# A batched matmul on one core: PSUM tiles at fixed banks, and one row of a store moved between DMA engines

## The chip, the cores and the metric

One core of a Trainium2 chip. The metric is the device time of one execution in microseconds (us), median of several; the profile's span is about 1.8 us shorter than the timed execution it belongs to.

## The reference

```python
# x: 32 x 256 x 512 fp32, y: 32 x 512 x 384 fp32
def reference(x, y):
    return np.einsum('bij,bjk->bik', x, y).astype(np.float32)
```

## The kernel before

The 32 batches go in eight groups of four. For each group the kernel loads x (2 MB) and y (3 MB), rounds both to fp16 and transposes x on VectorE, multiplies on TensorE, copies the result out of PSUM (mostly on ScalarE) and stores 1.5 MB. The order of the parts is a fixed plan (x and y are loads, T rounds and transposes x, R rounds y, M multiplies, C and D copy the result out on ScalarE and VectorE, S stores), and all DMAs are issued from one queue, that of the sync engine. In the code below cuts are marked with `...`, and some statements that stand on several lines are joined.

```python
PLAN = """
x0 x1 y0
T0 x2 y1
...                                             # cut
T6 D4 R5 M5 C5 y7
T7 D5 R6 M6 C6 R7 M7 C7 D7 S3 S4 S5 S6 S7
"""
...
    psum_pool = ctx.enter_context(
        tc.tile_pool(name="psum", bufs=2 * Q, space=bass.MemoryType.PSUM)    # Q = 4: eight tiles
    )
...
    def multiply(n):
        ...
        for e in range(NE):                     # NE = 2
            for g in range(Q):
                ps_of[n, e, g] = psum_pool.tile([P, K], F32, name="o_ps")
            for t in range(T):                  # T = 16
                for g in range(Q):
                    s = slice(g * PQ, (g + 1) * PQ)
                    keep(nc.tensor.matmul(ps_of[n, e, g], xt[s, e, t // 2, :, t % 2], y_r[s, t],
                                          start=(t == 0), stop=(t == T - 1)))
...
    def store(n):
        w = width(n)
        per = P // w
        o = o_of.pop(n).rearrange("p (u f) k -> p u f k", u=Q // per)
        for u in range(Q // per):
            b = n * Q + u * per
            keep(nc.sync.dma_start(
                out=out[b : b + per].rearrange("g (s f) k -> (g s) f k", s=w), in_=o[:, u]))
```

A store of groups 0 to 5 is one DMA: 128 partitions, from each a run of eight rows of 384 fp32 (8 x 1.5 KB = 12 KB). Groups 6 and 7 are stored in two DMAs each, of 6 KB runs.

Of the kernel before, what the change touches and what calls it, by code (L numbers as in the profile page):

```python
# [1 line left out]

# [4 lines left out]


MM_DT = mybir.dt.float16
F32 = mybir.dt.float32  # L10
P = 128


Q = 4
STEP = 4
O_BUFS = 5
WIDE_GROUPS = 6



# [4 lines that stand above are left out]
T1 R0 M0 C0 x3 y2  # L25
T2 D0 R1 M1 C1 x4 y3 S0
T3 D1 R2 M2 C2 x5 y4 S1
T4 D2 R3 M3 C3 x6 y5
T5 D3 R4 M4 C4 x7 y6 S2
T6 D4 R5 M5 C5 y7  # L30
T7 D5 R6 M6 C6 R7 M7 C7 D7 S3 S4 S5 S6 S7
"""


@with_exitstack
def kernel(
    ctx: ExitStack,
    tc: tile.TileContext,
    x: bass.AP,
    y: bass.AP,  # L40
    out: bass.AP,
):
    nc = tc.nc

    B, I, J = x.shape
    _, _, K = y.shape

    PQ = P // Q
    R = I // PQ
    T = J // PQ  # L50
    TW = T // 2
    NE = I // P
    N = B // Q

    x_pool = ctx.enter_context(tc.tile_pool(name="x_pool", bufs=2))
    y_pool = ctx.enter_context(tc.tile_pool(name="y_pool", bufs=2))
    xr_pool = ctx.enter_context(tc.tile_pool(name="xr_pool", bufs=1))
    xt_pool = ctx.enter_context(tc.tile_pool(name="xt_pool", bufs=3))
    yr_pool = ctx.enter_context(tc.tile_pool(name="yr_pool", bufs=2))
    o_pool = ctx.enter_context(tc.tile_pool(name="o_pool", bufs=O_BUFS))  # L60
    psum_pool = ctx.enter_context(
        tc.tile_pool(name="psum", bufs=2 * Q, space=bass.MemoryType.PSUM)
    )

    keep = tc.keep_in_program_order




    x_of, y_of, xt_of, yr_of, ps_of, o_of = {}, {}, {}, {}, {}, {}  # L70

    def width(n):
        return PQ if n < WIDE_GROUPS else 2 * PQ

    def on_vector(n, e, g):
        if n < WIDE_GROUPS:
            return (e, g) == (NE - 1, Q - 1)
        return n == N - 1 and g % 2 == 1

    def load_x(n):  # L80
        x_of[n] = x_pool.tile([P, R, J], F32, name="x_sb")
        keep(
            nc.sync.dma_start(  # L83
                out=x_of[n],
                in_=x[n * Q : (n + 1) * Q].rearrange("g (p r) j -> (g p) r j", r=R),
            )
        )

    def load_y(n):
        y_of[n] = y_pool.tile([P, T, K], F32, name="y_sb")  # L90
        keep(
            nc.sync.dma_start(
                out=y_of[n],
                in_=y[n * Q : (n + 1) * Q].rearrange("g (q t) k -> (g q) t k", t=T),
            )
        )

    def transpose_x(n):


        x_r = xr_pool.tile([P, R, J], MM_DT, name="x_r")
        keep(nc.vector.tensor_copy(x_r, x_of.pop(n)))  # L102
        xt_of[n] = xt_pool.tile([P, NE, TW, P], F32, name="xt_sb")
        b = width(n) // PQ
        src = x_r.bitcast(F32).rearrange("p (b h e) (q t) -> p b e t h q", b=b, e=NE, t=TW)
        dst = xt_of[n].rearrange("p e t (h s b) -> p b e t h s", s=PQ, b=b)
        for e in range(NE):
            for c in range(b):
                keep(nc.vector.transpose(dst[:, c, e], src[:, c, e]))  # L109

    def round_y(n):
        y_sb = y_of.pop(n)
        yr_of[n] = yr_pool.tile([P, T, K], MM_DT, name="y_r")
        for a in range(0, T, STEP):
            keep(nc.vector.tensor_copy(yr_of[n][:, a : a + STEP], y_sb[:, a : a + STEP]))  # L115

    def multiply(n):
        xt = xt_of.pop(n).bitcast(MM_DT).rearrange("p e t (m c) -> p e t m c", c=2)
        y_r = yr_of.pop(n)
        o_of[n] = o_pool.tile([P, R, K], F32, name="o_sb")  # L120
        for e in range(NE):
            for g in range(Q):
                ps_of[n, e, g] = psum_pool.tile([P, K], F32, name="o_ps")
            for t in range(T):
                for g in range(Q):
                    s = slice(g * PQ, (g + 1) * PQ)
                    keep(
                        nc.tensor.matmul(  # L128
                            ps_of[n, e, g],
                            xt[s, e, t // 2, :, t % 2],  # L130
                            y_r[s, t],
                            start=(t == 0),
                            stop=(t == T - 1),
                        )
                    )

    def collect(n, vector):
        w = width(n)
        per = P // w
        copy = nc.vector.tensor_copy if vector else nc.scalar.copy  # L140
        o = o_of[n].rearrange("p (u f) k -> p u f k", u=Q // per)
        for e in range(NE):
            for g in range(Q):
                if on_vector(n, e, g) != vector:
                    continue
                ps = ps_of.pop((n, e, g))
                a = g % per * w
                for h in range(per):
                    keep(copy(o[a : a + w, g // per, h * NE + e], ps[h * w : (h + 1) * w]))  # L149
# [4 lines that stand above are left out]
        o = o_of.pop(n).rearrange("p (u f) k -> p u f k", u=Q // per)  # L154
        for u in range(Q // per):
            b = n * Q + u * per
            keep(
                nc.sync.dma_start(  # L158
                    out=out[b : b + per].rearrange("g (s f) k -> (g s) f k", s=w),
                    in_=o[:, u],  # L160
                )
            )

    parts = {
        "x": load_x,
        "y": load_y,
        "T": transpose_x,
        "R": round_y,
        "M": multiply,
        "C": lambda n: collect(n, False),  # L170
        "D": lambda n: collect(n, True),
        "S": store,
    }
    for step in PLAN.split():
        parts[step[0]](int(step[1:]))


# [1 line left out]
_INS = ['x', 'y']  # L179
_OUTS = [((32, 256, 384), 'float32')]  # L180


# [23 lines left out]
```

## Time and profile before

| | before |
|---|---|
| median of 3 runs, us | 135.07 (135.02 to 135.42) |
| busiest engine | VectorE (DVE), 72% of the span |
| data DMA queue, of 16 engines' span | 96.8% |
| moved by that queue | 54.5 MB |

How to read it: here the DMA engines are full from the second slice to the last but one (share 1.01 from 10 to 120 us), so the time is bytes over rate (54.5 MB at 409 GB/s are 133.3 us), and that share stood although the compute engines waited (TensorE 59.8 us for VectorE). But the sixteen DMA engines don't stop together. The mean share hides which of them ends last, and the last one sets the end: the last landing is at 132.30 us, and the sync engine's wait of 7.1 us ends there. The landing times of a DMA (sixteen for one of 128 partitions, read here as one for each engine, when its share of the data has arrived) show that. Below, an engine's lateness is its landing time after that of the first engine of the same DMA, and the spread is the lateness of the last. In this trace the spread, once there, stays: 2.54 us in the load that lands from 88.4 us, 2.53 in the last store, from 129.8. And the instruction transfers share the engines with the data: between 20 and 110 us 16 data packets are in flight at 91% of the moments without such a transfer, and 15 at 91% of those with one.

### The profile page before, as it was taken

What the parts mean: (1) busy time and instruction counts of PE and PEld (TensorE: products, weight loads), DVE (VectorE), ACT (ScalarE), POOL (GpSimd) and SP (SyncE); (2) the same over time, 40 slices, a digit from 0 to 9 for tenths busy, and PEclk for the clock granted to TensorE, in tenths of its full rate; (3) what the DMA queues carried; (4) which work ended last, traced back from release to release, by engine and by line L of the source; (5) the groups of instructions that cost most, each with busy time, mean ns of one, the idle gap of its engine ahead of it and who ended that gap; (6) DMA issues with size and microseconds to landing.
All of it is one profiled execution on the core that took longest, in us unless ns stands there. A gap on an engine that the chain in (4) does not pass through costs nothing.

```text
span 133.3 us, 2445 instructions
## 1 busy us (share of the span) xinstructions
PE 60.5 (45%) x1024; PEld 37.4 (28%) x1024; DVE 96.1 (72%) x92; ACT 91.5 (69%) x193; POOL 0.2 (0%) x4
## 2 busy tenths in 40 slices
PE   0000004970398039907980079700992298787000
PEld 0000002540255025503550045400560296444000
DVE  0049999699969999999069990899999940765300
ACT  3000000099999999999999993999959999997200
POOL 0000000000000000000000000000000000000000
PEclk9999999998569855995599555995599658999655
DMA  5999999989999999999999999999999999999992
GB/s 103 433 413 443 450 425 408 489 384 440 411 462 443 391 443 408 417 407 443 435 430 418 431 404 450 440 425 428 472 391 388 479 428 391 424 439 411 411 409 94
DMA packets 3755, 54.68 MB, mean 410 GB/s; under 512 B 416, under 2 KB 416, under 8 KB 928
## 3 DMA queue, kind: packets, MB, share of 16 engines
q1 hardware_dynamic: 3744, 54.53, 96.8%
q8 instruction: 8, 0.13, 0.4%
q14 instruction: 3, 0.02, 0.0%
HBM read 41.94 MB, written 12.58 MB: 409 GB/s over the span
## 4 chain that ended last, share of the span: by engine, by line
DMA 39%; DVE 21%; PE 16%; ACT 14%; issue 1%; DVEq 0%; SPq 0%
DMA x_sb<-in_x_dram 39%; PE o_ps L128 16%; ACT o_sb L149 14%; DVE xt_sb L109 7%; DVE o_sb L149 6%; DVE x_r L102 5%; DVE y_r L115 2%; DVEq L201 0%; SPq L158 0%; DVEq L102 0%; SPq L83 0%
## 5 line engine op out<-in xcount | busy, mean ns | idle before, releaser
L149 ACT COPY o_sb<-o_ps 32x384 f32<-32x384 f32 (+1 forms) x192 | 90.2, 470 | 31.9 <-PE o_ps L128 27.4
L128 PE MATMUL o_ps<-y_r,xt_sb 32*128 32x384 f16 x1024 | 60.5, 396 | 61.8 <-DVE y_r L115 59.8
L128 PEld LDWEIGHTS <-xt_sb 32*128 32x128 f16 x1024 | 37.4, 112 | 84.6 <-issue 52.6
L115 DVE CAST y_r<-y_sb 128x1536 f16<-128x1536 f32 x32 | 28.5, 953 | 6.1 <-DMA y_sb<-in_y_dram 5.9
L102 DVE CAST x_r<-x_sb 128x4096 f16<-128x4096 f32 x8 | 18.4, 2294 | 19.3 <-DMA x_sb<-in_x_dram 19.2
L109 DVE STREAM_TRANSPOSE xt_sb<-x_r 128x1024 f32<-128x1024 f32 (+1 forms) x20 | 31.6, 1627 | 0.3
L149 DVE COPY o_sb<-o_ps 32x384 f32<-32x384 f32 (+1 forms) x32 | 17.8, 556 | 2.9 <-PE o_ps L128 1.4
L149 ACT ACT_TABLE_LOAD x1 | 1.3, 1283 | 0.7 <-PEq L190 0.7
L190 POOL MEMSET const-bfloat16-1.0<- 128x1 bf16 x1 | 0.1, 103 | 0.0
L190 POOL MEMSET const-uint8-127<- 128x1 uint8 x1 | 0.1, 101 | 0.0
L190 POOL MEMSET const-float32-0.0<- 128x1 f32 x1 | 0.1, 98 | 0.2 <-issue 0.2
L190 POOL MEMSET const-float32-1.0<- 128x1 f32 x1 | 0.1, 98 | 0.0
## 6 DMA issues: line engine op xcount, KB each, us to landing
y_sb<-in_y_dram SPq DMA_DIRECT2D x8, 3072.0 KB, 22.3
x_sb<-in_x_dram SPq DMA_DIRECT2D x8, 2048.0 KB, 22.4
out_dram<-o_sb SPq DMA_DIRECT2D x6, 1536.0 KB, 23.7
out_dram<-o_sb SPq DMA_DIRECT2D x4, 768.0 KB, 8.4
```

The lines of the kernel that those rows point to most:

```text
L102: keep(nc.vector.tensor_copy(x_r, x_of.pop(n)))
L109: keep(nc.vector.transpose(dst[:, c, e], src[:, c, e]))
L115: keep(nc.vector.tensor_copy(yr_of[n][:, a : a + STEP], y_sb[:, a : a + STEP]))
L128: nc.tensor.matmul(ps_of[n, e, g], xt[s, e, t // 2, :, t % 2], y_r[s, t], start=(t == 0), stop=(t == T - 1),)
L149: keep(copy(o[a : a + w, g // per, h * NE + e], ps[h * w : (h + 1) * w]))
L190: nc = _bacc.Bacc("TRN2", target_bir_lowering=False, num_devices=1)
```

## The change

The intent: PSUM tiles are bound to fixed banks in place of a rotating pool, and in the store of group 5 (the sixth) some bytes are moved from six DMA engines to ten others.

```diff
+UNEVEN = 5
...
-        tc.tile_pool(name="psum", bufs=2 * Q, space=bass.MemoryType.PSUM)
+        tc.tile_pool(name="psum", bufs=1, space=bass.MemoryType.PSUM)
...
+    bank = {
+        (e, g): psum_pool.tile([P, K], F32, name=f"o_ps_{e}_{g}") for e in range(NE) for g in range(Q)
+    }
...
-                ps_of[n, e, g] = psum_pool.tile([P, K], F32, name="o_ps")
+                ps_of[n, e, g] = bank[e, g]
...
+            dst = out[b : b + per].rearrange("g (s f) k -> (g s) f k", s=w)
+            if n != UNEVEN:
+                keep(nc.sync.dma_start(out=dst, in_=o[:, u]))
+                continue
+
+            keep(nc.sync.dma_start(out=dst[:, : R - 1], in_=o[:, u, : R - 1]))
+            keep(nc.sync.dma_start(out=dst[:100, R - 1], in_=o[:100, u, R - 1]))
+            keep(nc.sync.dma_start(out=dst[100:, R - 1], in_=o[100:, u, R - 1]))
```

The traces number no engine, so the numbers 0 to 15 are names: 0 to 9 for the ten engines on which the DMA of 100 partitions lands, 10 to 13 for the four more of the fourteen on which the DMA of 28 partitions lands, 14 and 15 for the other two. That a name means the same engine in another run is assumption.

More of the change, by code (lines that the diff above doesn't have):

```diff
@@ L156, in store @@
             b = n * Q + u * per
-            keep(
-                nc.sync.dma_start(
-                    out=out[b : b + per].rearrange("g (s f) k -> (g s) f k", s=w),
-                    in_=o[:, u],
-                )
-            )
+            dst = out[b : b + per].rearrange("g (s f) k -> (g s) f k", s=w)
[5 more added lines that the diff above has]
+            keep(nc.sync.dma_start(out=dst[100:, R - 1], in_=o[100:, u, R - 1]))
     parts = {
```

## The prediction

> **What bounds the kernel now.** I read the page first, for the engines and for the DMA row, then the table by stretch (busy time by window) over the whole run and finely over its end, then the wait lists and the order in which the DMAs are issued, and last the trace's own records of DMA packets and of landings.
>
> The page of the kernel before:
>
> ```profile
> span 133.3 us, 2445 instructions
> ...
> PE 60.5 (45%) x1024; PEld 37.4 (28%) x1024; DVE 96.1 (72%) x92; ACT 91.5 (69%) x193; POOL 0.2 (0%) x4
> ...
> DMA  5999999989999999999999999999999999999992
> ...
> q1 hardware_dynamic: 3744, 54.53, 96.8%
> q8 instruction: 8, 0.13, 0.4%
> ...
> HBM read 41.94 MB, written 12.58 MB: 409 GB/s over the span
> ```
>
> No compute engine is busy for more than 72% of the span. The DMA row is full in nearly every slice but the first and the last, and the one data queue took 96.8% of sixteen engines' span. So the end is set by bytes over DMA rate: 54.5 MB at 409 GB/s is the span. The second queue line is small but matters below: eight transfers of instructions ride on the same sixteen DMA engines.
>
> The table by stretch, over the run and then over the end (columns: stretch, its length, PE, PEld, DVE, ACT and POOL busy with counts, granted clock, mean DMA share, GB/s):
>
> ```profile
> 10.00:30.00 20.00, 7.08 (x128) 4.28 (x128) 18.64 (x12) 3.44 (x8) 0.00 (x0) 1.00 1.01 433
> 60.00:90.00 30.00, 16.69 (x256) 9.44 (x256) 21.66 (x20) 27.00 (x58) 0.00 (x0) 0.72 1.01 431
> ```
>
> ```profile
> 128.00:129.00 1.00, 0.00 (x0) 0.00 (x0) 0.00 (x0) 0.00 (x0) 0.00 (x0) 0.50 1.04 436
> 129.00:130.00 1.00, 0.00 (x0) 0.00 (x0) 0.00 (x0) 0.00 (x0) 0.00 (x0) 0.50 0.85 356
> 130.00:130.50 0.50, 0.00 (x0) 0.00 (x0) 0.00 (x0) 0.00 (x0) 0.00 (x0) 0.50 0.68 283
> 130.50:131.00 0.50, 0.00 (x0) 0.00 (x0) 0.00 (x0) 0.00 (x0) 0.00 (x0) 0.50 0.42 172
> 131.00:131.50 0.50, 0.00 (x0) 0.00 (x0) 0.00 (x0) 0.00 (x0) 0.00 (x0) 0.50 0.29 123
> 131.50:132.00 0.50, 0.00 (x0) 0.00 (x0) 0.00 (x0) 0.00 (x0) 0.00 (x0) 0.50 0.06 25
> ```
>
> In the body all sixteen engines are full (share 1.0). At the end they don't stop together: the share falls from 1.04 to 0.06 over some 2.5 us. This tail is what the change can work on. The trace's landing records say the same: the last store's sixteen completions, one for each engine, come 0, 0.06, 0.13, 0.18, 0.59, 0.90, 1.30, 1.41, 1.49, 1.55, 1.56, 1.82, 2.04, 2.11, 2.41 and 2.53 us after the first of them (129.78 us), so the last is at 132.30 and their mean at 131.04. The first load's sixteen lie within 0.77 us. The late ones appear one at a time through the run, and in the landing records a new engine about 1.5 us late turns up just after several of the eight 16 KB instruction transfers (30.2, 44.2, 58.0, 71.6, 86.1, 101.5, 115.6 and 123.8 us, each about 1.0 us long). [...] The trace does not number the engines.
>
> The wait list of the sync engine's queue from 90 us, and its order of issues:
>
> ```profile
> SPq L158 <- ACT o_sb L149: 14.2, 3, 7.1
> SPq L158 <- DVE o_sb L149: 11.6, 3, 7.3
> ...
> SPq L201 <- DMA out_dram<-o_sb: 7.1, 1, 7.1
> ```
>
> ```profile
> 96.38 28.73 SPq L158 DMA_DIRECT2D out_dram<-o_sb  x7
> ```
>
> The last store is issued at about 125.1 us and then waited for 7.1 us. While the stores waited for results, the DMA share stayed at 1.0 (0.98 in 120 to 130 us): a backlog of several us stands ahead of each store, so issue time and compute are hidden even at the end.
>
> [...] The trace before has only 128-row transfers (3,744 packets are 26 x 16 x 9)[...]. [...] here a 16 KB packet takes 0.611 us, 26.8 GB/s. [...]
>
> **The change part by part.**
>
> Fixed PSUM banks: before, a pool of eight buffers handed out in the order e, g, with eight tiles a group; so tile (e, g) already came back to the same buffer each group. The instruction order on PE, ACT and DVE is the same in both builds. At most the waits for a free buffer are written otherwise; the profile before has only 1.8 us of PE waiting for ACT, and compute is off the path. Cost 0.
>
> The store of group 5 (1.5 MB, 12 KB from each of 128 partitions, eight rows of 1.5 KB) becomes three DMAs: seven rows for all partitions (10.5 KB each, sixteen engines, eight packets each), the last row of 100 partitions on engines 0 to 9 (ten packets each), and of 28 partitions on engines 0 to 13 (two each). Bytes for each engine: before 96 KB; after 84 + 15 + 3 = 102 KB on 0 to 9, 87 KB on 10 to 13, 84 KB on 14 and 15.
>
> Packet times in the trace: 12 KB 0.460 us and 6 KB 0.234 us, each starting 4 ns before the end of the one ahead, so 0.456 and 0.230: 0.226 for 6 KB and 4 ns fixed. Estimates from these: a 10.5 KB packet 0.400, a 1.5 KB packet 0.0605.
> - Engines 0 to 9: 8 x (0.400 - 0.456) + 12 x 0.0605 + 2 semaphore packets of 0.005 = -0.45 + 0.73 + 0.01 = **+0.29 us**.
> - Engines 10 to 13: -0.45 + 2 x 0.0605 + 0.005 = **-0.32 us**.
> - Engines 14, 15: **-0.45 us**.
>
> Mean: about +0.05 us, ((10 x 0.29 - 4 x 0.32 - 2 x 0.45) / 16), the price of 128 more data packets and 24 more semaphore packets. On the sync queue two issues are added, 2 x 0.35 us (the issue rows' 0.332 to 0.506), beside the 7 us of backlog: 0 on the path. The end moves by what happens to whichever engine is last.
>
> If engines 14 and 15 are the two at 2.41 and 2.53, and 10 to 13 the next four, the last becomes 2.53 - 0.45 = 2.08 (engines 0 to 9 reach 1.56 + 0.29 = 1.85): **-0.45 us**. If the last engine is one of 0 to 9: **+0.29 us**. If 14 and 15 are last but one at 2.11 is among 0 to 9, that one reaches 2.40: **-0.13 us**. The uneven split only makes sense if somebody saw the high-numbered engines lag, so I give the first and third cases together 0.7, the second 0.3. The centre is 0.35 x -0.45 + 0.35 x -0.13 + 0.3 x 0.29 = -0.12 us. From 135.07 that is 134.95.
>
> **The rivals.**
> - *The wrong engines.* The lag sits on engines that get more bytes, and the time rises to about 135.4. For: eight fetches hit perhaps eight different engines, and only six are spared. Against: the intent of the split.
> - *Short packets are dear.* A 1.5 KB run into HBM could cost much more than 0.06 us; at 0.2 us twelve of them would add 12 x 0.14 = 1.7 us and give 136.8. Against: the fixed part between 6 and 12 KB is 4 ns.
> - *A new wait on the queue.* Two more DMAs shift the rotation of the eight completion counters: in the changed build the last stores wait for the counters of the loads and stores eight places before, y7 (landed at 114.0) and S3 (117.7), and both land before the last stores are issued at 120 to 125 us. So hidden, 0.
> - *Compute ends later or earlier through the banks.* Nothing in the wait lists says so, and 7 us of backlog would hide a few tenths either way.
> - *The lag changes from run to run.* The three times before, 135.02, 135.07 and 135.42, spread more than my whole expected effect; then the change is not seen.
>
> **Range and chances.** The mechanism gives -0.45 to +0.29 us, and run-to-run spread adds some 0.2. I predict 134.95 us, 134.5 to 135.5. Two per cent is 2.7 us, more than the whole tail of 2.5 us, and perfect levelling would give only 132.30 - 131.04 = 1.26 us. So faster by over 2% is 0.005; slower by over 2% needs the dear packets or something unseen, 0.01; within 2% 0.985.
>
> **What would show it.** Right: the data queue still at about 97% of sixteen engines' span; packets of 1.5 KB near 0.065 us; landings of the two small DMAs on ten and fourteen engines; the last store's landings spread over some 2.1 to 2.4 us in place of 2.53. Wrong engines: a spread of about 2.8 us. Wrong about packets: 1.5 KB packets of 0.15 us and more. Wrong about the backlog: a DMA share below 0.9 somewhere in 100 to 128 us, or PE and ACT ending later than the 122 to 125 us of before.

## The result, and the profile after

The changed kernel takes 135.06 us (median of 6 runs, 134.60 to 135.59), the kernel before 135.22 us (6 runs, 135.02 to 135.42). The ratio is 0.9989, 95% interval 0.9965 to 1.0013, which holds 1: the same. (A ratio is the mean time of one kernel's runs over that of the other's of the same rounds, so not quite the ratio of the medians. Executions over 1.5% slower than the fastest of the same kernel are left out of the means.)

The page of the changed kernel:

```profile
span 133.2 us, 2445 instructions
...
DMA  5999999999999999999999999999999999999992
...
DMA packets 3907, 54.68 MB, mean 411 GB/s; under 512 B 440, under 2 KB 568, under 8 KB 1080
...
q1 hardware_dynamic: 3896, 54.53, 96.8%
```

The bytes and the share of the data queue are unchanged. The counts of sizes are cumulative: 568 - 440 = 128 packets are the new 1.5 KB rows.

The table by stretch of the changed kernel at its end (same columns and stretches as in the prediction):

```profile
128.00:129.00 1.00, 0.00 (x0) 0.00 (x0) 0.00 (x0) 0.00 (x0) 0.00 (x0) 0.50 1.04 436
129.00:130.00 1.00, 0.00 (x0) 0.00 (x0) 0.00 (x0) 0.00 (x0) 0.00 (x0) 0.50 0.90 375
130.00:130.50 0.50, 0.00 (x0) 0.00 (x0) 0.00 (x0) 0.00 (x0) 0.00 (x0) 0.50 0.73 307
130.50:131.00 0.50, 0.00 (x0) 0.00 (x0) 0.00 (x0) 0.00 (x0) 0.00 (x0) 0.50 0.50 209
131.00:131.50 0.50, 0.00 (x0) 0.00 (x0) 0.00 (x0) 0.00 (x0) 0.00 (x0) 0.50 0.12 49
131.50:132.00 0.50, 0.00 (x0) 0.00 (x0) 0.00 (x0) 0.00 (x0) 0.00 (x0) 0.50 0.03 12
```

The tail is a little fuller until 131 us (0.50 against 0.42) and emptier after (0.12 against 0.29): in this execution the engines stop closer together. The order of issues on the sync engine's queue after (start, length, line), and the wait at the end:

```profile
96.48 0.90 SPq L164 DMA_DIRECT2D out_dram<-o_sb  x2
111.14 0.33 SPq L167 DMA_DIRECT2D out_dram<-o_sb  x1
111.64 0.78 SPq L168 DMA_DIRECT2D out_dram<-o_sb  x1
112.48 0.80 SPq L169 DMA_DIRECT2D out_dram<-o_sb  x1
117.53 7.48 SPq L164 DMA_DIRECT2D out_dram<-o_sb  x4
```

```profile
SPq L208 <- DMA out_dram<-o_sb: 7.1, 1, 7.1
```

The two small DMAs took 0.78 and 0.80 us to issue, the even one 0.33. They are issued at 111 to 113 us and their data moves at 121 to 124 us; the last issue ends at 125.0 us (before 125.1), and the wait behind it is 7.1 us as before.

The landing records of the two traces, us after the first engine, sorted (they carry no engine number):

```
before, store of group 5:            0 0.06 0.12 0.13 0.18 0.59 0.91 1.23 1.41 1.50 1.57 1.82 1.96 2.13 2.38 2.53
before, last store (first 129.78):   0 0.06 0.13 0.18 0.59 0.90 1.30 1.41 1.49 1.55 1.56 1.82 2.04 2.11 2.41 2.53
after, seven rows of group 5:        0 0.07 0.26 0.30 0.47 0.93 1.22 1.42 1.46 1.58 1.60 1.67 1.81 1.92 2.40 2.78
after, last store (first 130.00):    0 0.02 0.14 0.24 0.26 1.02 1.17 1.25 1.25 1.36 1.44 1.51 1.52 1.62 1.73 2.10
```

In the changed kernel the spread falls from 2.78 to 2.10 us across the split store; the last landing is at 132.10 us, before at 132.30. The two small DMAs landed on ten and on fourteen engines: their 128 packets run in ten rows of ten and fourteen rows of two, and ten of the fourteen begin within 10 ns of the end of a row of ten. Matching their landings with those of the seven rows tells the groups apart: engines 0 to 9 were 0, 0.07, 0.26, 0.30, 1.22, 1.42, 1.46, 1.58, 1.60 and 1.67 us late, 10 to 13 were 0.47, 1.92, 2.40 and 2.78, and 14 and 15 were 0.93 and 1.81. All 128 packets of 1.5 KB took 0.065 us, and the median packet of 10.5 KB 0.404.

### The profile page after: what moved, and what is told of

It reads as the page before. It is cut to its first block, busy times and chain, and to the rows that moved or that the text cites. A ratio compares the mean times of both kernels' runs of the same rounds, so it can differ in the third digit from the quotient of the medians.

```text
span 133.2 us, 2445 instructions
## 1 busy us (share of the span) xinstructions
PE 59.9 (45%) x1024; PEld 33.9 (25%) x1024; DVE 96.1 (72%) x92; ACT 91.7 (69%) x193; POOL 0.2 (0%) x4
## 3 DMA queue, kind: packets, MB, share of 16 engines
q1 hardware_dynamic: 3896, 54.53, 96.8%
## 4 chain that ended last, share of the span: by engine, by line
DMA 39%; DVE 21%; PE 16%; ACT 15%; issue 1%; DVEq 1%; SPq 0%
DMA x_sb<-in_x_dram 39%; PE o_ps L133 16%; ACT o_sb L154 15%; DVE xt_sb L114 7%; DVE o_sb L154 6%; DVE x_r L107 5%; DVE y_r L120 2%; DVEq L208 1%; SPq L164 0%; DVEq L107 0%; SPq L88 0%
## 5 line engine op out<-in xcount | busy, mean ns | idle before, releaser
L133 PE MATMUL o_ps<-y_r,xt_sb 32*128 32x384 f16 x1024 | 59.9, 394 | 62.3 <-DVE y_r L120 60.4
L133 PEld LDWEIGHTS <-xt_sb 32*128 32x128 f16 x1024 | 33.9, 112 | 88.0 <-DVE y_r L120 41.2
```

## The experiments

Theory A: the end moves only as the load of the slowest DMA engine moves, by the step sizes of the prediction. Rival B: the banks do something. Rival C: there is no effect to be seen in the time.

### Each part alone

`e1_banks_only` is the changed kernel with the split off:

```diff
-UNEVEN = 5
+UNEVEN = None
```

> Fixed PSUM banks alone, store of group 5 in one DMA as before. Theory A (the split of the store does all there is): last store's sixteen landings spread over about 2.5 to 2.8 us as before, ratio to before 1.000 +- 0.002. Rival B (the banks do it): spread 2.1 us as in the changed kernel, ratio about 0.999. Rival C (nothing real): ratio 1.000 here and in the next run alike, but then the spreads should not separate either.

Measured: 135.20 us (5 runs) against 134.95 (11 runs), ratio 1.0018, interval 1.0006 to 1.0031. The last store's landings spread over 2.78 us, with no narrowing. The banks don't narrow it, and rival B falls. There is a warning in this run: its DMAs, matmuls and copies are those of the kernel before in the same order, and still its interval excludes 1. What differs in the traces is how waits are written (three semaphore instructions on TensorE in place of ten), so either the banks cost 0.2% or this is drift, and no run tells which. The kernel before had medians of 135.22, 134.95 and 134.99 us in its three sets of rounds, which is also 0.2%, so the intervals below say less than they seem to at that size.

`e2_split_only` is the change with the rotating pool put back:

```diff
-        tc.tile_pool(name="psum", bufs=1, space=bass.MemoryType.PSUM)
+        tc.tile_pool(name="psum", bufs=2 * Q, space=bass.MemoryType.PSUM)
...
-                ps_of[n, e, g] = bank[e, g]
+                ps_of[n, e, g] = psum_pool.tile([P, K], F32, name="o_ps")
```

> The split store alone, PSUM from the pool as before. Theory A: before the split (landings of the store of group 4) a spread of about 2.5 to 2.8 us, after it 2.1 to 2.3, the last engine 0.32 + 0.29 us nearer to the first; ratio about 0.998, between 0.996 and 1.000. Rival B: spread unchanged, ratio 1.000.

Measured: 135.10 us (6 runs, 134.78 to 135.59) against 134.95, ratio 1.0008, interval 0.9990 to 1.0026. The expected narrowing did not come: ahead of the split the spread was only 1.82 us in this execution, its latest engine was one of 0 to 9, which get more, and the spread at the end was 1.87. So which engine is last is not always the same, and a fixed split can narrow the spread in some executions only.

### A larger dose

`e3_two_rows` and `e4_all_rows` put two and all eight rows of each run into the two small DMAs:

```diff
-            keep(nc.sync.dma_start(out=dst[:, : R - 1], in_=o[:, u, : R - 1]))
-            keep(nc.sync.dma_start(out=dst[:100, R - 1], in_=o[:100, u, R - 1]))
-            keep(nc.sync.dma_start(out=dst[100:, R - 1], in_=o[100:, u, R - 1]))
+            keep(nc.sync.dma_start(out=dst[:, : R - 2], in_=o[:, u, : R - 2]))      # not in e4
+            keep(nc.sync.dma_start(out=dst[:100, R - 2 :], in_=o[:100, u, R - 2 :]))  # R - 8 in e4
+            keep(nc.sync.dma_start(out=dst[100:, R - 2 :], in_=o[100:, u, R - 2 :]))
```

> Changed kernel with the last TWO rows of each run in the two small DMAs. Theory A, from the landings of the changed kernel ahead of the split (engines 0 to 9 at most 1.67 us behind the first, the worst of 10 to 13 at 2.78, the worst of 14 and 15 at 1.81) and 0.06 + 0.226 us a row on 0 to 9, -0.33 on 10 to 13, -0.45 on 14 and 15: ends at max(1.67 + 0.51, 2.78 - 0.67, 1.81 - 0.9) = 2.18 on the old zero, so 0.6 us earlier than without a split, ratio about 0.9955; landings after the split spread over 2.18 - 0.51 = 1.7 us. Rival (short packets or more DMAs cost what the split saves): no faster than the changed kernel, ratio 0.999 or more.

> Changed kernel with all EIGHT rows of the store of group 5 in the two small DMAs, 100 partitions on engines 0 to 9 and 28 on 0 to 13. Theory A: engines 0 to 9 carry 144 KB in place of 96, +1.87 us, so the worst of them ends at 1.67 + 1.87 = 3.54 against 2.78 without a split: 0.75 us later, ratio about 1.0055; engines 14 and 15 come first at the end. Rival (the total of bytes sets the end, not the slowest engine): the same bytes, ratio 1.000.

Measured: two rows 135.68 us, ratio 1.0059 (1.0031 to 1.0087), slower where 0.9955 was expected; eight rows 140.38 us (median of 6 with one slow run of 142.10; 140.20 without it), ratio 1.0381 (1.0342 to 1.0421), where 1.0055 was expected. Both miss by far, so there is a cost that the sum lacks. The table by stretch shows it. The changed kernel:

```profile
123.00:125.00 2.00, 0.00 (x0) 0.00 (x0) 1.52 (x3) 1.08 (x3) 0.00 (x0) 0.81 1.01 412
125.00:127.00 2.00, 0.00 (x0) 0.00 (x0) 0.00 (x0) 0.00 (x0) 0.00 (x0) 0.50 1.03 427
```

The eight-row run:

```profile
119.00:121.00 2.00, 2.00 (x55) 1.48 (x50) 1.64 (x3) 1.74 (x4) 0.00 (x0) 1.00 1.04 373
121.00:123.00 2.00, 0.62 (x13) 0.19 (x5) 1.33 (x3) 1.44 (x4) 0.00 (x0) 1.00 0.99 337
123.00:125.00 2.00, 0.00 (x0) 0.00 (x0) 0.89 (x2) 0.46 (x1) 0.00 (x0) 1.00 1.09 326
```

The engines are as busy as ever (0.99 to 1.09) and move a fifth less: 326 in place of 412 GB/s. Single packets take longer. From 118 to 129 us 70 packets ran more than 1.2 times their usual length, 29.5 us too long in sum; a 12 KB packet, usually 0.460 us, took up to 1.95. In the two-row run the same happens to 15 packets between 121 and 127 us, 3.0 us in sum (3 KB packets of up to 0.661 us against a median of 0.121); several of these fall beside an instruction transfer at 122.9 us, and one engine was 4.0 us behind the first at the end. That profile is of the slowest of the six executions (136.61 us; the fastest took 135.21), so it shows what can happen rather than the usual case. In the changed kernel no packet between 121 and 125 us was slow.

### What makes packets slow

Two things differ between the eight-row run and the kernel before: the load of the engines, and the cut of the partitions. That another cut pairs engines with partitions differently was assumption; no trace shows which partition a packet reads. `c1_even_96_32` keeps the load of each engine even (planned as eight 12 KB packets each) and changes only the cut:

```diff
-            keep(nc.sync.dma_start(out=dst[:, : R - 1], in_=o[:, u, : R - 1]))
-            keep(nc.sync.dma_start(out=dst[:100, R - 1], in_=o[:100, u, R - 1]))
-            keep(nc.sync.dma_start(out=dst[100:, R - 1], in_=o[100:, u, R - 1]))
+            keep(nc.sync.dma_start(out=dst[:96], in_=o[:96, u]))
+            keep(nc.sync.dma_start(out=dst[96:], in_=o[96:, u]))
```

> Changed kernel, but the whole store of group 5 goes by two even DMAs, 96 partitions on 16 engines (six each) and 32 on 16 (two each): each engine has eight 12 KB packets as in the kernel before[...]. Theory (the dear packets of the two-row and eight-row runs come from the other pairing of engines and partitions[...]): 12 KB packets over 0.55 us are seen by the dozen between 119 and 128 us, several us in sum, and the time is 0.5 to 2% longer. Rival (they come from the unequal load on fewer engines): all 12 KB packets at 0.46 us, ratio 1.000.

Measured: runs of 136.06, 136.07 and 137.28 us (a fourth, 140.61, is slow and left out) against 134.99, ratio 1.0114, interval 1.0073 to 1.0155. The same stretch in this run:

```profile
121.00:123.00 2.00, 1.21 (x29) 0.60 (x21) 0.78 (x2) 1.25 (x3) 0.00 (x0) 1.00 1.02 375
123.00:125.00 2.00, 0.00 (x0) 0.00 (x0) 1.45 (x3) 1.01 (x3) 0.00 (x0) 0.90 0.92 304
```

Between 118 and 127 us 31 packets were slow, 12.9 us in sum. The load is planned even and all sixteen engines are used, so unequal load seems not to be needed: it was enough to cut the partitions 96 to 32. The spread of the landings, 2.21 us at the store of group 4, was 3.20 us at the end. What in the cut makes packets slow was not shown.

`e5_two_groups` moves as many bytes between engines as the two-row run, but in 1.5 KB packets:

```diff
-UNEVEN = 5
+UNEVEN = (4, 5)
...
-            if n != UNEVEN:
+            if n not in UNEVEN:
```

> The one-row split of the change on the stores of group 4 and of group 5: the same bytes moved between engines as in the two-row run, but all short packets of 1.5 KB. Theory (levelling works, and the two-row run lost by slow 3 KB packets): no short packet over 0.08 us, 0 to 9 at most 1.7 + 0.58 = 2.28, the worst of 10 to 13 at 2.7 - 0.64 = 2.06: end 0.4 us before that of the kernel before, ratio 0.997. Rival (unequal loads don't help whatever the packets): ratio 1.003 or more, as the two-row run had 1.0059.

Measured: 135.00 us (6 runs) against 134.99, ratio 1.0011, interval 0.9989 to 1.0032. Between 118 and 126 us, where the short rows and most of both stores move, seven packets were slow, 0.8 us in sum, and the longest of 1.5 KB took 0.174 us, where none over 0.08 was expected. Most of the loss of the two-row run is gone, but the expected 0.3% did not appear either. The trace shows one reason: in this execution the two latest engines ahead of the first split (2.21 and 2.23 us) were among 0 to 9, which get more, and the spread at the end was 3.08 us. (It was the slowest of the six executions, 135.46 us.)

### Which engines are late

Four probes of one execution each cut the last row so that the lists of landings peel off one engine number at a time (the DMAs of 75, 28, 13 and 12 partitions land on 15, 14, 13 and 12 engines):

```diff
-            keep(nc.sync.dma_start(out=dst[:100, R - 1], in_=o[:100, u, R - 1]))
-            keep(nc.sync.dma_start(out=dst[100:, R - 1], in_=o[100:, u, R - 1]))
+            c = 0
+            for rows in (75, 28, 13, 12):     # (12, 88, 10, 18), (96, 8, 7, 12, 5), (112, 7, 4, 3, 2)
+                keep(nc.sync.dma_start(out=dst[c : c + rows, R - 1], in_=o[c : c + rows, u, R - 1]))
+                c += rows
```

> A probe, not a version: the last row of group 5's store goes by DMAs of 75, 28, 13 and 12 partitions, so on 15, 14, 13 and 12 engines. The engines missing from one landing list to the next are numbers 14, 13 and 12, and 15 is in none. Theory A (which engines are late is the same in each execution, the worst among 10 to 15 as in the profile after): at least two of 12 to 15 are among the four latest ahead of the split. Rival (the instruction transfers land on other engines in each execution): 12 to 15 are spread over the whole list, with no more than chance would give, one of the four latest.

> The same probe with 12, 88, 10 and 18 partitions: 12, 11, 10 and 9 engines, which tells engines 11, 10 and 9 one by one. Theory A: two of 9 to 13 are more than 2 us late, as in the profile after. Rival: none or another count, and the sets of this probe and the one before cannot be put together.

> The same probe for low numbers: 96 partitions on 16 engines, then 8, 7, 12 and 5 partitions on 8, 7, 12 and 5 engines. Theory A: the four or five engines that are not late at all are the same ones each time, and lie below 10, so at least two of 0 to 4 are within 0.5 us of the first. Rival: not so.

> The same probe for the lowest numbers: 112 partitions on 16 engines, then 7, 4, 3 and 2 partitions on 7, 4, 3 and 2 engines. Theory A: the lateness of engines 0 to 4 agrees with the probe before within 0.3 us. Rival: it differs by more than 1 us for at least one of them.

Measured (135.19, 134.60, 134.89 and 135.14 us, one run each; 135.34 for the kernel before). The numbers are the best fit of the landing lists. Refitted one list at a time, they leave 1 to 31 ns of mean misfit for a landing; only the list of 12 partitions in the third probe fits loosely (88 ns), and nothing in the table rests on it:

| engines | lateness ahead of the split, us |
|---|---|
| 12 | 2.60 (first probe) |
| 13 and 14 | 1.86 and 1.91 (first) |
| 15 | 0.63 (first) |
| 11, 10, 9 | 2.16, 0.04, 1.49 (second) |
| 0 to 4 | 0.03, 0.11, 1.22, 1.26, 1.71 (third) |
| 0 and 1; 2; 3 | 0.11 and 1.15; 0; 1.08 (fourth) |
| 4 to 6 | 1.55, 1.71, 1.82 (fourth) |

The first probe's forecast held: three of engines 12 to 15 are among its four latest. In the second, engine 11 is over 2 us late and the other such engine (2.49 us) is one of 12 to 15, so its forecast of two among 9 to 13 is possible but not shown. In the third two of engines 0 to 4 are within 0.5 us of the first, as forecast, and the fourth agrees with it on these engines as a set, within the 0.3 us expected. No probe numbers all sixteen, but the latest engine was one of 12 to 15 in the first two, and not one of 0 to 7 in the third or of 0 to 6 in the fourth; in the profile after it was one of 10 to 13. The exceptions are the split-only run (latest 1.82 us, one of 0 to 9; 10 to 13 at 1.64 to 1.77) and the run of two groups above. So theory A's pattern holds mostly, not always.

### Giving less to engines 11 to 15

`v1_121_7` uses this:

```diff
-            keep(nc.sync.dma_start(out=dst[:100, R - 1], in_=o[:100, u, R - 1]))
-            keep(nc.sync.dma_start(out=dst[100:, R - 1], in_=o[100:, u, R - 1]))
+            keep(nc.sync.dma_start(out=dst[:121, R - 1], in_=o[:121, u, R - 1]))
+            keep(nc.sync.dma_start(out=dst[121:, R - 1], in_=o[121:, u, R - 1]))
```

> A version: the last row goes by 121 partitions on engines 0 to 10 and 7 on engines 0 to 6, so that 11 to 15, among them the four latest (11 to 14 in the probes), lose 12 KB each. Theory: the worst goes from about 2.7 us to 2.25, engines 0 to 6 to at most 1.75 + 0.27 = 2.0; spread at the end about 2.0 us, end 0.45 us before that of the kernel before, ratio 0.9965 (0.9945 to 0.999). Rival (which engine is last changes too much from run to run): ratio 0.999 to 1.001.

Measured: 135.28 us (6 runs, 134.88 to 135.68) against 134.99, ratio 1.0024, interval 1.0002 to 1.0045. In its profile the split did what was expected: the spread fell from 2.46 to 1.82 us and the last landing was at 132.01 us (132.30 before). But the profiled execution was the fastest of the six (134.88 us); the others took up to 135.68, so a good profile of one execution was not the kernel's usual one. No version here beats the kernel before in the same rounds; the changed kernel was not run again in them.

Set side by side, the profiles show what the split does to the landings. Where the engines that get less included the latest, the spread narrowed from the split store to the last one: 2.78 to 2.10 us after, 2.46 to 1.82 in this run, 2.49 to 2.02 in the second probe, whose last row goes nearly all to engines 0 to 10. Where the row is not split it hardly changed (2.53 to 2.53 before, 2.85 to 2.78 with the banks only), nor in the other three probes, which deal the row out more evenly (2.60 to 2.52, 2.53 to 2.45, 2.67 to 2.54). Where the latest engine was among those that get more, it stayed or grew (1.82 to 1.87, and 2.23 to 3.08 with two groups). In the half-matmul run below (2.60 to 2.57) the latest got less, but one of 0 to 9 was 2.24 us late and took its place. The last landing came at 131.87 to 132.10 us in the three that narrowed and at 132.23 to 132.48 in the five that hardly changed. These are single executions; in the medians of several runs no gain is clear of noise.

### What makes engines late

`h1_half_matmuls` gives a wrong result: half the matmuls are left out (512 in place of 1,024), and the data DMAs are the same.

```diff
-            for t in range(T):
+            for t in range(0, T, 2):
...
-                            stop=(t == T - 1),
+                            stop=(t == T - 2),
```

> WRONG RESULT ON PURPOSE: the changed kernel with every second step of the contraction left out, 512 matmuls and 512 weight loads in place of 1,024 each; all DMAs as in the changed kernel. Theory (the instruction transfers make single DMA engines late, about 1.5 us for each of the eight): four of 16 KB in place of eight, four engines fewer late by over 0.9 us ahead of the split (7 or 8 in place of about 11), mean lateness at the last store 0.4 us less (4 x 1.5 / 16), the end 0.3 to 0.9 us earlier, ratio 0.994 to 0.998. Rival (the engines are late for another reason, such as the memory): the same number of late engines, ratio 0.999.

The page of this run:

```profile
span 133.2 us, 1421 instructions
PE 47.9 (36%) x512; PEld 19.3 (14%) x512; DVE 96.0 (72%) x92; ACT 91.7 (69%) x193; POOL 0.2 (0%) x4
...
q8 instruction: 4, 0.07, 0.2%
```

Four instruction transfers are left of eight. The landing lists of the two kernels show engines late just after a transfer. In this run all sixteen engines are within 0.55 us until 37.7 us, and the first late one, 1.73 us, stands in the list of 44.4 to 46.2 us, after the first transfer at 40.5. In the kernel before, the first transfer is at 30.2 us and the first late engine, 1.85 us, already in the list of 32.2 to 34.1. Just after the transfer one data packet took 0.47 us more than usual in this run and 0.51 in the kernel before. With the transfer's own 1.1 us that is about the lateness.

How much they add up to is less clear. At the seven rows of group 5 eight engines were over 0.9 us late and the mean lateness was 0.95 us; with all eight transfers it was nine to eleven engines and 1.01 to 1.25 us (at the store of group 5 in the kernel before, the changed one, banks only, split only, the four probes and the 121 and 7 version). At the last store, for which 0.4 us less was expected, the mean was 1.08 us, against 1.04 in the profile after and 1.26 before: that forecast missed. And the latest engine was 2.60 us late all the same, and the time was 135.35 us, ratio 1.0045 (1.0021 to 1.0069): slower, which I cannot explain. Here too the profiled execution was the fastest of the six (135.01 us, others up to 135.90), so what its slower ones lost is in no trace.

How one engine gets 2.6 us late with half the transfers can be followed in its landing lists: 1.7 us after the transfer at 40.5 us, and 2.5 us in the load whose landings begin at 56.7 us, about when the first store starts to move. The kernel before has the same step: its two latest engines go from 1.8 and 1.9 to 2.3 and 2.5 us there. The stretches of the kernel before around it:

```profile
50.00:54.00 4.00, 4.00 (x67) 2.18 (x63) 3.89 (x4) 3.88 (x9) 0.00 (x0) 0.65 1.01 432
54.00:57.00 3.00, 2.39 (x57) 1.49 (x49) 3.00 (x2) 2.90 (x8) 0.00 (x0) 1.00 0.98 389
60.00:64.00 4.00, 3.04 (x39) 1.63 (x43) 3.42 (x4) 3.88 (x9) 0.00 (x0) 0.50 1.02 438
```

Busy engines move 389 in place of 432 GB/s; two 24 KB packets at 56.2 us took 0.77 and 0.95 us more than their usual 0.912. The store alone is not the cause, since slow load packets are seen from 55.1 us (54.2 in the changed kernel) and the first packet of the store starts at 56.3. Nor does the step always come: the split-only run has slow loads from 54.4 us too, but its two latest engines go from 1.21 and 1.27 to 1.03 and 1.06 us, and it is the profile with the least spread ahead of the split. What slows these loads is open. Halving the instruction transfers did not lower the maximum (2.60 us at the seven rows of group 5, against 2.53 at the store of group 5 before and 2.78 in the profile after), and the maximum sets the end.

## Why the prediction was right

The forecast of no visible change held, and what the split does to the landings is as predicted. The size did not get tested: the range of 134.5 to 135.5 us holds the time of the kernel before as well, so a change without any effect would have fallen in it too, and that 135.06 lies near 134.95 is partly luck.

- *What bounds the kernel*: right. Share of the data queue 96.8% before and after, the last wait 7.1 us before and after. That the bound is the latest of sixteen engines, not their mean, is how the landing lists read; the dose runs agree in direction for the eight rows, but their size is mostly the slow packets (29.5 us too long in sum).
- *Packet costs*: right. Estimated starts 0.0605 and 0.400 us apart, which with the 4 ns overlap are 0.065 and 0.404 us; measured exactly these. The rival of dear short packets falls for 1.5 KB in the changed kernel; single ones took up to 0.174 and 0.201 us in the runs of two groups and of 121 and 7. It holds for longer ones: the two-row run had 3 KB packets of up to 0.661 us.
- *The steps for each group of engines*: right in the profile after. The latest engine, one of 10 to 13, should come nearer to the first, one of 0 to 9, by 0.32 + 0.29 = 0.61 us; the spread went from 2.78 to 2.10, by 0.68.
- *Which engine is last*: the case I had written with the largest gain, engines 14 and 15 last, did not occur. Three of the four latest were among 10 to 13, so the relief for the last was 0.32 us, not 0.45. That case, one of 10 to 13 last, is not among the three that were weighed. In the split-only run the latest was among 0 to 9, which is the prediction's second case. Weighing the cases gave -0.12 us; the medians differ by -0.16, the ratio of split-only points the other way, and neither is clear of noise.
- *Banks*: no narrowing, as predicted. Whether the cost is 0 is not shown: the banks alone had a ratio of 1.0018.
- *Issue*: the two small DMAs cost 0.78 and 0.80 us to issue, not 0.35; hidden, as predicted, behind the backlog.
- *The rotation of counters*: no new wait appears; y7 landed by 114.1 us and S3 by 117.9, and the last stores were issued at 117.5 to 125.0 us.
- *Backlog*: right. The DMA share between 100 and 128 us was never below 0.92 in stretches of 2 us, and PE and ACT ended no later than before.

Still open: what the slower executions of the half-matmul run and of the 121 and 7 version lost (only their fastest executions were profiled), whether the banks cost 0.2%, what slows loads at 54 to 57 us, and what places an instruction transfer on one engine rather than another.

## What to carry to other kernels

When a kernel is bound by DMA, look at the landings of its last store: the distance from the last engine to the mean is all that levelling can give, and here it was 1.26 us of 135 (the whole spread was 2.5). Before cutting a store otherwise to level it, test the cut with an even load: a cut into 96 and 32 partitions cost 1.1% by itself, more than levelling could win. And run a kernel that should be equal beside the others; here one with the same DMAs, matmuls and copies differed by 0.2%, which was the size of the effect sought.
